# A two-layer encoder trunk on one core: values of the grouped attention one step later, the cast of the last gate in one step with its product, part of a scaling on ScalarE

## The chip, the core and the metric

The kernel runs on one core of a Trainium2 chip. The metric is the device time of one execution in microseconds (us); the time of a kernel is the median of several executions. In the profile PE is TensorE (PEld its weight loads), DVE is VectorE, ACT is ScalarE, POOL is GpSimd and SP is SyncE, which only issues DMAs here.

## What is computed

512 tokens of width 1024 pass through two layers. Both normalize the stream, project it, attend, gate, project back and add the result to the stream:

```
for i in range(2):
    h = rmsnorm(x, norm_g[i]);  proj = h @ w_in
    if i == 0: o_mix = mixer_dilated(q, k, v)      # 3 groups x 8 heads, windows with dilation 1, 4, 16,
                                                   # mixed by a softmax of their log-sum-exps
    else:      o_mix = mixer_axial_gqa(q, k, v)    # 8 query heads, 2 key/value heads, axial rotary
    o_mem = memory_attention(q_mem, rmsnorm(mem))  # 4 heads over 256 memory tokens
    y = concat(o_mix, o_mem) * silu(gate);  x = x + y @ w_out[i]
```

Everything is float32. In layer 1's grouped attention each block of 128 query rows of a head sees all 512 keys.

## The kernel before

**Products.** Float32 accuracy is reached with three matmuls per product: each operand is split into a high part (a cast on ScalarE) and a low part (what is left, a subtraction on VectorE), and `mm3` (L163 to L166) adds high x high (L164), low x high (L165) and high x low (L166) in PSUM. The projections (`s_chunk`, L356) use a scheme in the manner of Strassen with seven instead of eight products of quarters, so that many sums and differences of weights, activations and results are formed on the other engines; L364 copies a product out on ScalarE, L375 and L381 combine products on VectorE.

**Weights.** The class `Weights` (L182) streams the weights in pieces of 128x1024 (512 KB). `dma` (L229) loads them on SP's queue, as many ahead as the table `KEEP` (L39) allows for the kind of the piece: W1b are the seven input projections of layer 1, W2b is the part of its output projection for the memory heads and heads 0 to 3, O1 the part for heads 4 to 7. `sum` (L243) forms sums of pieces by adding DMAs on POOL's queue (L252, L261, L266, L271), `hi` (L278) casts a piece on ScalarE (L287), `lo` (L292) subtracts on VectorE (L297). A cast is taken two slots after its load or sum was issued at the earliest. `advance` (L313) does some of each once per slot.

**The order of the work** is written out by hand. The class `Driver` (L42) counts slots: after every product of a projection TensorE's program calls `tick` (L94), which lets each waiting piece of other work (written as a generator) go one step. `first` work of a slot comes ahead, then generators that finish a product, then at most two steps of attention, and last what was put on the list `late`. `half` (L109) gives the attention a step in the middle of a product. All engines work through their instructions in the order in which they are issued here, and an instruction that waits holds what is behind it on its engine.

**Buffers.** `m4` (L141) hands out tiles of 128x1024 from a pool of 23, for the weights' pieces (wl), keys (kbT), values (vb), queries (qb), transposed probabilities (pbT), gate products (yf, y) and others. `s2` gives tiles of 128x512. Attention uses four PSUM banks (`at`, L150), the projections four (`pj`). A tile or a bank that is handed out again can be written only when its last reader is done.

**Layer 0's attention** (`attn_a`, L1058) works on one head at a time. Two sets of probabilities (o = 0, 1) are formed and multiplied in place by a factor c per row, in which the softmax over the groups lies: c is formed at L1148, `scale(o)` at L1154 to L1157 applies it with four instructions on VectorE, one for each block of 128 rows, and with a second factor of 0.5. Then `turn` (L1159) transposes the set on TensorE, and `pv` multiplies it with the values.

**Layer 1's attention** (`attn_b`, L1356) is a pipeline over 32 blocks of a head's 128 query rows. In a step t, block t has its scores (`score`), block t-1 its exponentials (ScalarE, L1372), t-2 is scaled by its sum (L1379), t-3 is transposed (`turn`, L1388), and the transposed block is cut into a high part (L1392, ScalarE) and a low part (L1397, VectorE). The two blocks of a pair share one pair of pbT tiles, which the first of them takes from the pool. When t-4 is the second block of a pair, `pv` multiplies the pair with the values into a PSUM tile ob, and `out_` copies it (L1413) to o. After two pairs the head is whole and is stored to DRAM (`put_ob`, L1278). The last line of `attn_b` gives the stages with their offsets.

**Gates** (`gates`, L747, for both layers) are three projections: for the memory heads (g = 0), heads 0 to 3 (g = 1) and heads 4 to 7 (g = 2). `ev` finishes a quarter: tanh on ScalarE (L768), the SiLU (L770), the load of the attention's output og (L763) as soon as it is stored, and the multiplication. For g < 2 this is L778 (to yf); `prep_y` (L794) makes the activations of the output projection from them later (casts at L805, subtractions at L806). For g = 2 it is L781, in the next slot the cast to the high part of y (L784), and in the one after it the subtraction for the low part (L786). Then `out_rest` (L728) can multiply these heads with their part of the output weights, the last work of a layer. In layer 1, the last heads' y is what the end of the kernel waits for, behind the attention's last block.

Of the kernel before, what the change touches and what calls it, by code (L numbers as in the profile page):

```python
# [12 lines left out]
AF = mybir.ActivationFunctionType  # L13
ALU = mybir.AluOpType
# [21 lines left out]

SEQ = [1, 2, 0] + list(range(3, len(PLAN)))
T1_DMA = 17
KEEP = {"T2": 8, "T2b": 4, "O1": 4, "W1": 9, "W2": 10, "W2s": 9, "W1b": 7, "W2b": 9}  # L39


class Driver:  # L42
# [83 lines left out]
def trunk_kernel(ctx: ExitStack, tc: tile.TileContext, x, mem, wall, norm_g, mem_norm_g, gcol,  # L126
                 qn_a, kn_a, qn_b, kn_b, ident_d, mask_d, tab_a, tab_b, out):
    nc = tc.nc
    V, A, G, T = nc.vector, nc.scalar, nc.gpsimd, nc.tensor
# [6 lines left out]
    drv = Driver()  # L136
# [610 lines left out]
    def gates(od, o_done):  # L747

        ys, yf, y_done, YW = [None] * 4, [None, None], set(), {}

        def gate(H, first, g, half=False):


            yt = [[m4(F32R, "y").rearrange("p (h t) -> p h t", h=2) for _ in range(2)] for _ in range(2)] if g == 2 else None
            if g < 2:
                yf[g] = [m4(name="yf") for _ in range(2)]

            def ev(q, u, t):
                i, j = int(q[0]) - 1, int(q[1]) - 1
                h0, ts = first + 2 * j, slice(i * 256, (i + 1) * 256)  # L760
                def load():
                    o = s2(name="og")
                    nc.sync.dma_start(o.rearrange("p (h t) -> p h t", h=2), od[h0:h0 + 2, :, ts].rearrange("h p t -> p h t"))  # L763
                    return o

                o = load() if {h0, h0 + 1} <= o_done else None
                th = s2(name="th")
                A.activation(th, t, AF.Tanh, scale=0.5)  # L768
                yield 1
                V.scalar_tensor_tensor(t, th, 1.0, t, ALU.add, ALU.mult)  # L770
                yield 1
                if not o:
                    while not {h0, h0 + 1} <= o_done:
                        yield 1
                    o = load()
                    yield 1
                if g < 2:
                    V.tensor_tensor(yf[g][j][:, i * 512:(i + 1) * 512], t, o, ALU.mult)  # L778
                    y_done.add((g, i, j))
                    return  # L780
                V.tensor_tensor(t, t, o, ALU.mult)  # L781
                yield 1
                tv = t.rearrange("p (h t) -> p h t", h=2)
                A.copy(yt[j][0][:, :, ts], tv)  # L784
                yield 1
                V.tensor_tensor(yt[j][1][:, :, ts], tv, yt[j][0][:, :, ts].bitcast(F32), ALU.subtract)  # L786
                y_done.add((g, i, j))
                if {(2, 0, j), (2, 1, j)} <= y_done:
                    for k in range(2):
                        ys[2 * j + k] = (yt[j][0][:, k], yt[j][1][:, k])  # L790

            s_chunk(256, H, ev, tokens=False, half=half, soon=g == 2)

        def prep_y():  # L794

            def wait(*gi):
                while not {(g, i, j) for g, i in gi for j in range(2)} <= y_done:
                    yield 1

            def put(k, src):  # L800
                t = big(F32R, "y" + k)
                for j in range(2):
                    js = slice(j * 512, (j + 1) * 512)
                    lo = t[:, 1024 + j * 512:1024 + (j + 1) * 512]
                    A.copy(t[:, js], src[j])  # L805
                    V.tensor_tensor(lo, src[j], t[:, js].bitcast(F32), ALU.subtract)  # L806
                YW[k] = t.rearrange("p (a k t) -> p a k t", a=2, k=4)

            while None in yf:
                yield 1  # L810
            a11, a21, a12, a22 = [[yf[g][j][:, i * 512:(i + 1) * 512] for j in range(2)] for g in range(2) for i in range(2)]
            yield from wait((1, 0))
            put("12", a12)
            yield 1
            yield from wait((0, 0))
            put("11", a11)
            yield 1
            yield from wait((0, 1), (1, 1))
            s1 = [s2(name="ys") for _ in range(2)]
            for j in range(2):  # L820
                V.tensor_tensor(s1[j], a21[j], a22[j], ALU.subtract)
            yield 1
            put("S1", s1)
            yield 1
            for j in range(2):
                V.tensor_tensor(s1[j], s1[j], a11[j], ALU.subtract)
            yield 1
            put("S2", s1)
            yield 2
            for j in range(2):  # L830
                V.tensor_tensor(a12[j], a12[j], s1[j], ALU.add)
            yield 1
            put("S4", a12)
            yield 1
            for j in range(2):
                V.tensor_tensor(a21[j], a11[j], a21[j], ALU.subtract)
            yield 1
            put("S3", a21)
            yield 2
            put("22", a22)  # L840

        return gate, prep_y, YW, ys
# [215 lines left out]
    def attn_a(h, qk0, qs, ks, v12, n_done):  # L1058
# [3 lines left out]
        prob = [m4(name="p").rearrange("p (b k) -> p b k", b=4) for _ in range(2)]  # L1062
# [10 lines left out]
        for o in range(2):  # L1073
            new = []
            for b2 in range(2):
                sp = at("sa").rearrange("p (b k) -> p b k", b=2)
                mine = []
                for i in range(2):
                    b = 2 * b2 + i
                    cs = slice(b * 128, (b + 1) * 128)  # L1080
                    if o == 0:
                        lo, hi = max(0, 128 * b - 64), min(S, 128 * b + 192)
                        c0 = lo - (128 * b - 64)
# [61 lines left out]
        rd = sm(8, "rd")  # L1145
        V.reciprocal(rd, dn)
        c = small.tile([128, 2, 4], F32, tag="c", name="c", bufs=2)
        V.tensor_tensor(c.rearrange("p o b -> p (o b)"), e[:, 0], rd, ALU.mult)  # L1148
        yield 1

        pts = {}
# [2 lines left out]
        def scale(o):  # L1154
            for b in range(4):
                c0, c1 = (64 if o == 0 and b == 0 else 0), (192 if o == 0 and b == 3 else 256)
                V.tensor_scalar(prob[o][:, b, c0:c1], prob[o][:, b, c0:c1], c[:, o, b:b + 1], 0.5, ALU.mult, ALU.mult)  # L1157

        def turn(o):  # L1159

# [195 lines left out]
    def attn_b():  # L1356
        sc, pr, pts, tp, rs, oo = {}, {}, {}, {}, {}, {}

        def score(i):
            h, b = divmod(i, 4)  # L1360
            qh, ql = qs_b[h // 4]
            cs = slice(b * 128, (b + 1) * 128)
            sc[i] = at("sb")
            mm3(sc[i], qh[h % 4 // 2][:, h % 2, cs], ql[h % 4 // 2][:, h % 2, cs], kbT[0][:, h // 4], kbT[1][:, h // 4], True, True)

        def top(i):
            pr[i] = sm(1, "nmb"), sm(1, "denb"), sm(1, "rdb"), s2(name="pb")
            V.tensor_reduce(pr[i][0], sc[i], axis=AX.X, op=ALU.max, negate=True)

        def exps(i):  # L1370
            nm, den, rd, pp = pr[i]
            A.activation(pp, sc.pop(i), AF.Exp, bias=nm, accum_out=den)  # L1372

        def recip(i):
            V.reciprocal(pr[i][2], pr[i][1])

        def scale(i):
            _, _, rd, pp = pr[i]
            A.activation(pp, pp, AF.Copy, scale=rd)  # L1379

        def turn(i):
            b2, j = divmod(i, 2)
            pp = pr.pop(i)[3]
            if j == 0:
                pts[b2] = [m4(F32R, "pbT").rearrange("p (k q) -> p k q", k=4) for _ in range(2)]
            tp[i] = at("ptb").rearrange("p (k q) -> p k q", k=4)
            for k in range(4):
                T.transpose(tp[i][:, k, :], pp[:, k * 128:(k + 1) * 128], ident)  # L1388

        def hi(i):  # L1390
            b2, j = divmod(i, 2)
            A.copy(pts[b2][0][:, :, j * 128:(j + 1) * 128], tp[i])  # L1392

        def lo(i):
            b2, j = divmod(i, 2)
            qs = slice(j * 128, (j + 1) * 128)
            V.tensor_tensor(pts[b2][1][:, :, qs], tp.pop(i), pts[b2][0][:, :, qs].bitcast(F32), ALU.subtract)  # L1397

        def pv(i):
            h, b = divmod(i, 4)  # L1400
            if b % 2:
                pT = pts.pop(i // 2)
                o = oo[i] = at("ob")[:, 0:256]
                es = slice(h // 4 * 128, h // 4 * 128 + 128)
                for k in range(4):
                    mm3(o, vb[0][:, k, es], vb[1][:, k, es], pT[0][:, k], pT[1][:, k], k == 0, k == 3)

        def out_(i):
            h, b = divmod(i, 4)
            if b == 1:  # L1410
                rs[h] = put_ob(h)
            if b % 2:
                A.copy(rs[h][:, (b - 1) * 128:(b + 1) * 128], oo.pop(i))  # L1413
            if b == 3:
                put_ob(h, rs[h])

        yield from pipeline(32, (0, score, 0), (4, pv, 0), (3, turn, 0), (2, scale, 0), (1, exps, 0),
                            (0, top, 1), (1, recip, 1), (3, hi, 1), (3, lo, 1), (4, out_, 1),
                            ready=lambda i: n_rot[0] >= 8 + i // 16 * 4)

    for kvh in range(2):
# [134 lines left out]
```

## Time and profile before

| | |
|---|---|
| three executions | 972.17, 972.54, 968.25 us, median 972.17 |
| profiled execution | 966.39 us |
| its span, first to last instruction | 964.6 us |
| granted clock of TensorE, mean | 0.998 |
| groups of weights' splitting on VectorE (L297) | 255 instructions, 314.2 us |
| weights' casts on ScalarE (L287) | 255 instructions, 269.2 us |
| data moved | 209.81 MB, mean 218 GB/s |

The busy time of an engine is the time in which it worked, whatever waited for it. A row of the timeline has the start, the duration, the engine and line, the operation with the tile that it writes and those that it reads, its shape, and in brackets the idle time of the engine ahead of it and what ended that. A row with x2 or x4 stands for so many equal instructions in a row. In the list of waits a row has the waiting engine, tile and line, what it waited for, and then the total, the number and the longest in us. A row of a window has its length and the busy times of PE, PEld, DVE, ACT and POOL with the number of their instructions, the granted clock, the DMA share and the rate. All durations come from the one profiled execution.

### The profile page before, as it was taken

How to read it: one execution, taken by the hardware profiler on the slowest of the kernel's cores; microseconds unless marked ns; L12 is line 12 of the kernel's file. 1: busy time of each engine (PE TensorE's matmuls, PEld its weight loads, DVE VectorE, ACT ScalarE, POOL GpSimd, SP SyncE). 2: the span in 40 equal slices, each digit the busy share in tenths (PEclk: the TensorE clock that was granted, in tenths of full speed). 3: DMA queues.
4: the chain of work that ended last, by engine and by line, in shares of the span. 5: the costliest groups of instructions: out<-in, count | busy, mean ns of one | idle time of the engine just before them, and what ended most of it. 6: DMA issues, size and time to landing. Idle time of an engine off the chain costs nothing.

```text
span 964.6 us, 16613 instructions
## 1 busy us (share of the span) xinstructions
PE 947.5 (98%) x5682; PEld 833.3 (86%) x5682; DVE 790.6 (82%) x1411; ACT 683.0 (71%) x1701; POOL 339.7 (35%) x482
## 2 busy tenths in 40 slices
PE   8999999999999999999999999999899999999998
PEld 5879888888888888888899997888899999998876
DVE  4898676888888888888797999879888997779873
ACT  5874689686868686868675767556778887878760
POOL 1512523556454545464726011323233231011011
PEclk9999999999999999999999999999999999999999
DMA  9799946869686868685858989969976696877744
GB/s 361 234 285 341 288 112 177 288 123 265 147 259 151 258 155 261 154 262 132 269 147 216 276 194 281 310 198 308 284 174 148 175 239 163 222 202 173 191 144 131
DMA packets 89130, 209.81 MB, mean 218 GB/s; under 512 B 25299, under 2 KB 36051, under 8 KB 89045
## 3 DMA queue, kind: packets, MB, share of 16 engines
q1 hardware_dynamic: 69892, 145.76, 43.6%
q0 software_dynamic: 17856, 60.83, 33.7%
q10 hardware_dynamic: 1296, 2.16, 0.6%
q8 instruction: 45, 0.74, 0.3%
q14 instruction: 41, 0.33, 0.1%
HBM read 157.27 MB, written 12.65 MB: 176 GB/s over the span
## 4 chain that ended last, share of the span: by engine, by line
PE 86%; DVE 8%; ACT 3%; DMA 2%; issue 1%; SPq 0%; DVEq 0%; ACTq 0%
PE pj L166 22%; PE pj L164 22%; PE pj L165 22%; DVE wo L297 3%; PE qT L571 2%; PE sa L1089 1%; PE oo L1191 1%; PE pt L1170 1%; PE sa L1085 1%; PE ptb L1388 1%; DMA og<-odb 1%; PE xT L475 1%; PE ob L165 1%; PE row L592 1%; PE ob L166 1%
## 5 line engine op out<-in xcount | busy, mean ns | idle before, releaser
L297 DVE TENSOR_TENSOR wo<-wl,wh 128x1024 fp32r<-128x1024 f32 x255 | 314.2, 1238 | 5.8 <-ACT wh L287 5.7
L287 ACT CAST wh<-wl 128x1024 fp32r<-128x1024 f32 x255 | 269.2, 1059 | 55.9 <-PE pj L166 33.7
L164 PE MATMUL pj<-wh,hS 128*128 128x512 f32 (+1 forms) x448 | 164.3, 367 | 0.0
L165 PE MATMUL pj<-wo,hS 128*128 128x512 f32 (+1 forms) x448 | 158.8, 355 | 4.4 <-DVE wo L297 4.4
L166 PE MATMUL pj<-wh,hS 128*128 128x512 f32 (+1 forms) x448 | 158.7, 354 | 0.0
L164 PE MATMUL pj<-wh,h 128*128 128x512 f32 (+1 forms) x336 | 122.4, 364 | 0.0
L166 PE MATMUL pj<-wh,h 128*128 128x512 f32 (+1 forms) x336 | 118.5, 353 | 0.0
L165 PE MATMUL pj<-wo,h 128*128 128x512 f32 (+1 forms) x336 | 118.4, 352 | 0.1
L424 POOL TENSOR_TENSOR rstd<-mse,half 128x4 f32<-128x4 f32 (+2 forms) x98 | 102.2, 1043 | 8.2
L165 PEld LDWEIGHTS pj<-wo,hS 128*128 128x128 f32 x448 | 85.7, 191 | 15.3 <-DVE wo L297 5.3
L166 PEld LDWEIGHTS pj<-wh,hS 128*128 128x128 f32 x448 | 85.5, 191 | 12.2
L164 PEld LDWEIGHTS pj<-wh,hS 128*128 128x128 f32 x448 | 85.5, 191 | 10.4 <-ACT sn L364 0.4
L364 ACT COPY sn<-pj 128x512 f32<-128x512 f32 x132 | 73.9, 590 | 22.8 <-PE pj L166 19.2
L423 POOL TENSOR_SCALAR mse<-hss 128x4 f32<-128x4 f32 (+1 forms) x86 | 44.1, 513 | 124.0 <-ACT junk L559 120.2
L559 ACT ACTIVATE junk<-sn 128x128 f32<-128x128 f32 x264 | 79.0, 308 | 1.7 <-DVE sn L375 1.7
L1033 POOL TENSOR_TENSOR ta<-sn,tabs 128x128 f32<-128x128 f32 (+1 forms) x64 | 37.0, 579 | 120.0 <-DVE sn L564 91.6
L381 DVE TENSOR_TENSOR sn<-pj,sn 128x512 f32<-128x512 f32 x99 | 67.5, 684 | 5.4 <-PE pj L166 5.0
L166 PEld LDWEIGHTS pj<-wh,h 128*128 128x128 f32 x336 | 63.5, 189 | 8.9
L165 PEld LDWEIGHTS pj<-wo,h 128*128 128x128 f32 x336 | 63.7, 190 | 8.0 <-DVE wo L297 0.8
L164 PEld LDWEIGHTS pj<-wh,h 128*128 128x128 f32 x336 | 63.7, 190 | 7.2
L271 POOL DMA_DIRECT2D wl<-wl x33 | 29.1, 881 | 115.3 <-DVE wo L297 64.4
L164 PE MATMUL pj<-hS,wh 128*128 128x256 f32 x192 | 55.9, 291 | 0.0
(231 smaller groups left out, 2464.3 us busy)
## 6 DMA issues: line engine op xcount, KB each, us to landing
wl<-in_wall_dram SPq DMA_DIRECT2D x222, 512.0 KB, 7.0
wl<-wl POOLq DMA_DIRECT2D x66, 512.0 KB, 6.2
wl<-in_wall_dram POOLq DMA_DIRECT2D x42, 512.0 KB, 8.4
acc<-sn POOLq DMA_DIRECT2D x16, 256.0 KB, 5.2
od<-o SPq DMA_DIRECT2D x12, 256.0 KB, 5.8
og<-od SPq DMA_DIRECT2D x12, 256.0 KB, 6.8
odb<-o SPq DMA_DIRECT2D x12, 256.0 KB, 3.0
og<-odb SPq DMA_DIRECT2D x12, 256.0 KB, 4.5
```

The lines of the kernel that those rows point to most:

```text
L164: T.matmul(o, lh, rh, start=start, stop=False, skip_group_check=True)
L165: T.matmul(o, lh, rl, start=False, stop=False, skip_group_check=True)
L166: T.matmul(o, ll, rh, start=False, stop=stop, skip_group_check=True)
L271: G.dma_start(self.tile[key], self.tile[c, "T2", x], accum_op=ALU.add)
L287: A.copy(wh, self.tile[self.items[i]])
L297: V.tensor_tensor(wo, self.tile[key], wh.bitcast(F32), ALU.subtract)
L364: A.copy(t, b)
L381: V.tensor_tensor(t, b, t, ALU.subtract if q == "12" else ALU.add)
L423: G.tensor_scalar(e, ss, EPS, None, ALU.add)
L424: G.tensor_tensor(r, e, half[:, 0:n], ALU.pow)
L559: A.activation(jk, p[:, j * 128:(j + 1) * 128], AF.Square, scale=QS, accum_out=ss[:, j:j + 1])
L1033: G.tensor_tensor(ta[:, 0:n], xn[:, 0:n, 0:32], ropeA[:, 0, b, s0:s0 + n], ALU.mult)
```

## The change

There are four parts. In `attn_b` the stages `pv` and `out_` come five steps after the scores instead of four. The limit of pieces in flight of the kind W1b falls from 7 to 6. In a gate with g = 2 the cast of the product is put on the list `late` of the slot in which the product is formed, and the `yield` between them goes, so the subtraction comes in the slot after it. In `attn_a` the factor 0.5 goes into c, `scale` has one factor instead of two, and for head 7 ScalarE applies it instead of VectorE.

```diff
-KEEP = {"T2": 8, "T2b": 4, "O1": 4, "W1": 9, "W2": 10, "W2s": 9, "W1b": 7, "W2b": 9}
+KEEP = {"T2": 8, "T2b": 4, "O1": 4, "W1": 9, "W2": 10, "W2s": 9, "W1b": 6, "W2b": 9}
...
                 V.tensor_tensor(t, t, o, ALU.mult)
-                yield 1
                 tv = t.rearrange("p (h t) -> p h t", h=2)
-                A.copy(yt[j][0][:, :, ts], tv)
+                drv.late(lambda: A.copy(yt[j][0][:, :, ts], tv))
                 yield 1
                 V.tensor_tensor(yt[j][1][:, :, ts], tv, yt[j][0][:, :, ts].bitcast(F32), ALU.subtract)
...
-        V.tensor_tensor(c.rearrange("p o b -> p (o b)"), e[:, 0], rd, ALU.mult)
+        V.scalar_tensor_tensor(c.rearrange("p o b -> p (o b)"), e[:, 0], 0.5, rd, ALU.mult, ALU.mult)
...
-                V.tensor_scalar(prob[o][:, b, c0:c1], prob[o][:, b, c0:c1], c[:, o, b:b + 1], 0.5, ALU.mult, ALU.mult)
+                if h == 7:
+                    A.activation(prob[o][:, b, c0:c1], prob[o][:, b, c0:c1], AF.Copy, scale=c[:, o, b:b + 1])
+                else:
+                    V.tensor_scalar(prob[o][:, b, c0:c1], prob[o][:, b, c0:c1], c[:, o, b:b + 1], None, ALU.mult)
...
-        yield from pipeline(32, (0, score, 0), (4, pv, 0), (3, turn, 0), (2, scale, 0), (1, exps, 0),
-                            (0, top, 1), (1, recip, 1), (3, hi, 1), (3, lo, 1), (4, out_, 1),
+        yield from pipeline(32, (0, score, 0), (5, pv, 0), (3, turn, 0), (2, scale, 0), (1, exps, 0),
+                            (0, top, 1), (1, recip, 1), (3, hi, 1), (3, lo, 1), (5, out_, 1),
```

## The prediction, made before the changed kernel had run

> **What bounds the kernel now.** I read the busy times and the chain that ended last on the page, then the waits of TensorE, then the timeline at each of these waits, and last the windows around the three places that the change touches.
>
> ```profile
> span 964.6 us, 16613 instructions
> PE 947.5 (98%) x5682; PEld 833.3 (86%) x5682; DVE 790.6 (82%) x1411; ACT 683.0 (71%) x1701; POOL 339.7 (35%) x482
> PE 86%; DVE 8%; ACT 3%; DMA 2%; issue 1%; SPq 0%; DVEq 0%; ACTq 0%
> ```
>
> TensorE multiplies for 947.5 of 964.6 us. The change takes no matmul away, so all it can win lies in 17.1 us, and much of that is the start and the end. The waits, with the total, the number and the longest:
>
> ```profile
> PE pj L165 <- DVE wo L297: 5.0, 4, 2.9
> PE row L592 <- DMA row<-in_mem_norm_g_dram: 2.4, 1, 2.4
> PE ob L165 <- DVE pbT L1397: 2.2, 2, 1.4
> PE pj L166 <- DVE y L786: 1.0, 1, 1.0
> ```
>
> These name the places: weights that VectorE has not yet split (L297), the low halves of the grouped attention's probabilities (L1397), and the low half of the last gated heads (L786). In order of time:
>
> ```profile
> 592.62 0.50 PE L165 MATMUL pj<-wo,yS 128*128 128x512 f32 x1 [0.57 <-DVE wo L297]
> 594.43 0.50 PE L164 MATMUL pj<-wh,yS 128*128 128x512 f32 x1 [0.39 <-DVE sn L381]
> 678.80 0.39 PE L165 MATMUL pj<-wo,hS 128*128 128x256 f32 x1 [2.85 <-DVE wo L297]
> 873.93 0.39 PE L165 MATMUL ob<-pbT,vb 128*128 128x256 f32 x1 [1.37 <-DVE pbT L1397]
> 912.06 0.38 PE L165 MATMUL ob<-pbT,vb 128*128 128x256 f32 x1 [0.87 <-DVE pbT L1397]
> 940.41 0.50 PE L166 MATMUL pj<-wh,y 128*128 128x512 f32 x1 [1.04 <-DVE y L786]
> ```
>
> The sum is made against the profiled execution, 966.39 us (span 964.6 and 1.79 around it). That is 5.78 under the median of 972.17, so I add the sum's difference to the median. About 0.5%, 4.9 us, is what a measurement here can tell from no change.
>
> **a. The last head's scaling on ScalarE.** In layer 0 the four scalings of each set of head 7 leave VectorE.
>
> ```profile
> 578.80:602.90 24.10, 22.88 (x104) 17.51 (x103) 23.35 (x45) 18.57 (x30) 3.46 (x4) 1.00 0.99 281
> 589.70 1.14 DVE L1157 TENSOR_SCALAR p<-p,c 128x256 f32<-128x256 f32 x4
> 597.23 1.07 DVE L1157 TENSOR_SCALAR p<-p,c 128x192 f32<-128x192 f32 x4
> L691 ACT ACTIVATE pm<-pm,rdm 128x256 f32<-128x256 f32 x32 | 14.6, 509 | 0.0
> 596.15 1.22 ACT L805 CAST yS<-yf 128x512 fp32r<-128x512 f32 x2 [2.29 <-DVE yf L836]
> ```
>
> The window's columns are its length, then PE, PEld, DVE, ACT and POOL busy. VectorE is busy 23.35 of 24.10 us, so it sets the two waits at 592.62 and 594.43 (0.57 + 0.39 = 0.96). Taking 1.14 off just ahead of them removes both: **-0.96** (bounds -0.96 and 0). What hides the other side is ScalarE's idle time, 24.10 - 18.57 = 5.53 us, one piece of it the 2.29 at 596.15. The same operation at the same size, L691, takes 509 ns, and eight make at most 4.07 us. If that cover went, the transposes of head 7 would come late by what does not fit; the values of head 7 are needed only one to three slots on, so I take nothing. The factor 0.5 moves into c, and the other heads' scalings lose their second operation: still one instruction each, in front of which nobody waits, so 0.
>
> [...]
>
> **b. The values one step later.** In the loop over 32 blocks (four of 128 query rows to a head) the values matmuls are issued in the step after the one in which they were. The two waits for L1397 go, because the low half has a step more: **-2.24** (1.37 + 0.87; bounds -2.24 and 0).
>
> **c. What the later values hold.** A pair of blocks has two transposed tiles, a high and a low one. Two pairs are now alive between the turn of the next pair and the values of the last. They come from the pool of 23 tiles that also holds the weights. I count, at step 13: keys 2, values 2, queries 6, weights 9, gate products 2, probabilities 2, which is 23, full; the change makes it 25. The lowered limit of W1b does not help there, since from step 12 on the pieces being loaded are W2b's, with their limit of 9. From step 17 to 23 two query tiles are gone and a gate tile is more: 24. So in the odd steps 13 to 23 a new tile waits until the next step's values have read the old one. One such wait stands in the trace of before, 0.47 us at 840.25. The steps as PE runs them (scores 831.58, values 832.28, transposes 833.71, half a product 834.07, scores 835.58, whole product 836.64 to 839.58):
>
> ```profile
> 831.58 0.40 PE L164 MATMUL sb<-kbT,qb 128*128 128x512 f32 x1
> 832.28 0.28 PE L164 MATMUL ob<-pbT,vb 128*128 128x256 f32 x1
> 833.71 0.60 PE L1388 MATMUL ptb<-ident,pb 128*128 128x128 f32 x4
> 834.07 0.37 PE L164 MATMUL pj<-hS,wh 128*128 128x256 f32 x1
> 835.58 0.40 PE L164 MATMUL sb<-kbT,qb 128*128 128x512 f32 x1
> 836.64 0.36 PE L164 MATMUL pj<-h,wh 128*128 128x256 f32 x1
> 839.58 0.40 PE L164 MATMUL sb<-kbT,qb 128*128 128x512 f32 x1
> 834.35 0.59 ACT L1392 CAST pbT<-ptb 128x512 fp32r<-128x512 f32 x1 [2.11 <-PE ptb L1388]
> 834.97 0.69 DVE L1397 TENSOR_TENSOR pbT<-ptb,pbT 128x512 fp32r<-128x512 f32 x1 [1.73 <-ACT pbT L1392]
> 840.25 0.69 DVE L778 TENSOR_TENSOR yf<-sn,og 128x512 f32<-128x512 f32 x1 [0.47 <-PE sb L165]
> 835.00:868.00 33.00, 33.00 (x257) 31.71 (x256) 23.96 (x40) 26.12 (x52) 4.07 (x5) 1.00 0.71 183
> ```
>
> Scores take 0.70, values 1.43, half a product 1.51, a whole one 2.94. A held L1397 stands for 1.51 + 0.70 + 1.43 = 3.64 us in a half step, 5.07 in a whole one, and behind it on VectorE stand the weights' L297 and the scores' maximum; behind a held L1392 on ScalarE stand the weights' casts L287. TensorE feels it through the four PSUM banks of the attention: two hold scores that ScalarE has not read, one the new values, so the next transposes need the bank of the last ones, and that is free only after L1392 and L1397. At step 13 both are held: 0.59 + 0.69 and a handover of about 0.07, 1.35 us. At 15, 17, 19, 21 and 23 the low half alone is: 0.69 and a handover, 0.75. That is 1.35 + 5 x 0.75 = **+5.10**. The trace of before has no such wait on the probabilities, so the bounds are far apart: 0, if the shortage falls on weight loads, which have time; and 5.10 + 5.07 = 10.2, if on top VectorE ends the stage one hold behind (below). I take the figure worked out from the rows.
>
> **d. The tail.** The last values move one slot back, behind a product, and so do the copy, the store, the load of og and the multiplication. The cast of the last gate (L784) now follows its multiplication in the same slot, and the subtraction comes one slot sooner after it.
>
> ```profile
> 929.21 0.40 PE L164 MATMUL pj<-wh,yS 128*128 128x512 f32 x1
> 931.96 0.39 PE L164 MATMUL pj<-wh,y 128*128 128x512 f32 x1
> 936.05 1.36 DVE L781 TENSOR_TENSOR sn<-sn,og 128x512 f32<-128x512 f32 x2 [4.06 <-DMA og<-odb]
> 936.78 1.29 ACT L784 CAST y<-sn 128x512 fp32r<-128x512 f32 x2 [0.81 <-DVE sn L781]
> 937.33 1.22 DVE L297 TENSOR_TENSOR wo<-wl,wh 128x1024 fp32r<-128x1024 f32 x1
> 938.46 1.28 DVE L375 TENSOR_TENSOR sn<-sn 128x512 f32<-128x512 f32 x2
> 939.67 1.29 DVE L786 TENSOR_TENSOR y<-sn,y 128x512 fp32r<-128x512 f32 x2
> ```
>
> The product behind which they move takes 931.96 - 929.21 = 2.75. The multiplication waits for og (4.06), so it comes 2.75 later. The weights' L297 that stood between it and L786 goes ahead of it, into the wait: 938.46 - 937.33 = 1.13 less. The two L375 stay between, and under them the casts. L786 comes 2.75 - 1.13 = 1.62 later, TensorE needs it when it does now, and its wait grows from 1.04 to 2.66: **+1.62** (bounds -1.04, the whole wait gone, and +2.75). In layer 0 the same cast edit meets no wait of TensorE for L786 (the one in the list is at 940.41): 0.
>
> **e. One W1b piece fewer.**
>
> ```profile
> wl<-in_wall_dram SPq DMA_DIRECT2D x222, 512.0 KB, 7.0
> ```
>
> Each load for layer 1's input projections is issued one slot later on SP's queue, and the sums behind it on POOL's. A load lands in 7.0 us, some 2.4 slots of 2.94, and of the list's four waits for L297 the one at 678.80 is the last, so layer 1's weights come in time. I take **0**; the bound above is one slot at the layer change, +2.94.
>
> **Sum:** -0.96 - 2.24 + 5.10 + 1.62 + 0 = +3.52: 969.9 for the profiled execution, 972.17 + 3.52 = **975.7** on the median.
>
> **The rivals.**
>
> R1, slower: VectorE loses more than the banks show. The holds of 835 to 892 add up to 3 x 3.64 + 3 x 5.07 = 26.1 us, and VectorE has only 33.00 - 23.96 = 9.04 spare in 835 to 868. It can lag TensorE by one step only, since the hold ends with that step. From the point at which this lag eats the lead of the weights' splitting, TensorE waits for L297 too, by one hold: c becomes 10.2, the time 972.17 - 3.20 + 1.62 + 10.2 = 980.8. For it: VectorE's load. Against it: the splitting runs up to two slots ahead.
>
> [...]
>
> R2, the gains are kept: the pool's shortage falls on loads with time to spare, c is 0, and the time 972.17 - 3.20 + 1.62 = 970.6; if the tail's wait also goes, 972.17 - 3.20 - 1.04 = 967.9. For it: one tile is given back by W1b; the pool waits of before cost TensorE nothing. Against it: my count of 25.
>
> R3, the weights come late: one slot at the layer change on top, 975.7 + 2.94 = 978.6. For it: the 2.85 at 678.80 shows no slack in that place.
>
> R4, the later step does not do what it says:
>
> ```profile
> 868.00:892.20 24.20, 22.83 (x144) 20.21 (x144) 23.84 (x39) 21.58 (x41) 3.71 (x5) 1.00 0.71 175
> ```
>
> VectorE is full there (23.84 of 24.20), so the two waits of b come back as waits for something else of VectorE's: 975.7 + 2.24 = 977.9.
>
> **How the numbers follow.** Forecast 0.36, R1 0.20, R2 0.22 (0.06 of it at 967.9), R3 0.10, R4 0.12. Faster means under 967.3, slower over 977.0. Under 967.3 lies the lower edge of R2, with noise of the runs: 0.08. Over it lie R1, most of R3 and R4, and little of the forecast: 0.34. Within: 0.58. The forecast's own range is 973 to 978; from 968 to 981 all cases but the outer halves of R1 and of R2's lower branch are in.
>
> **What would show it.** a: no wait at 592 and 594, L1157 on ScalarE. b: no wait of ob for L1397. c: L1392 and L1397 waiting for ob's matmuls, and ptb for L1397, every second step from about 835; without such rows c is wrong and R2 holds. Waits for L297 between 835 and 892 speak for R1, one that is longer near 679 for R3. d: L786's wait about 2.7. It would be wrong altogether if the time fell under 968, which needs c at nothing and the tail's wait gone.

## The result and the profile after

The changed kernel takes 979.59 us (median of 6 executions, 977.57 to 980.30), the kernel before 970.23 us beside it (6 executions, 968.09 to 974.64). The ratio is 1.0095, with a 95% interval of 1.0068 to 1.0122: slower, by about 9.2 us. The prediction's number was 975.7. The time lies in its wide range of 968 to 981, but outside the forecast's own 973 to 978, and above 977.0, the side to which the prediction gave 0.34. The profiled execution of the changed kernel took 979.55 us. Line numbers of the changed kernel differ by one or two from those before: L1399 is the low half of the probabilities (before L1397), L1394 the high half (L1392), L1390 the transposes (L1388), L785 the low half of y (L786).

From the page of the changed kernel, the span and the busy times:

```profile
span 977.8 us, 16614 instructions
PE 952.3 (97%) x5682; PEld 836.6 (86%) x5682; DVE 788.9 (81%) x1403; ACT 685.3 (70%) x1709; POOL 341.3 (35%) x482
```

TensorE has the same 5682 matmuls and is busy 4.8 us longer (952.3 against 947.5); a part of them, behind the layer change, ran at a lower clock (0.50 from 688.5 to 694.5, below). The rest of the 13.2 us between the two spans is idle time of TensorE. Its waits (total, number, longest):

```profile
PE pj L165 <- DVE wo L297: 6.2, 4, 2.9
PE pj L164 <- ACT hS L539: 3.6, 1, 3.6
PE ptb L1390 <- DVE pbT L1399: 3.6, 5, 1.3
...
PE pj L164 <- DVE sn L381: 1.4, 2, 1.1
PE pj L166 <- DVE y L785: 1.1, 1, 1.1
```

Two large groups are new: the wait for hS, which is ScalarE's cast of layer 1's first activations, and the five waits of the transposes for L1399. The waits for L381 have grown from 0.4 to 1.4 us, and three single waits of 0.4 to 0.8 us are new too. The two waits of the values (ob) for the low half are gone, the wait for L785 at the end is there still. The timeline puts them in place:

```profile
581.21 0.50 PE L165 MATMUL pj<-wo,y 128*128 128x512 f32 x1 [1.80 <-DVE wo L297]
...
597.14 0.50 PE L164 MATMUL pj<-wh,yS 128*128 128x512 f32 x1 [1.08 <-DVE sn L381]
...
680.53 0.39 PE L165 MATMUL pj<-wo,hS 128*128 128x256 f32 x1 [2.87 <-DVE wo L297]
688.63 0.55 PE L164 MATMUL pj<-wh,hS 128*128 128x256 f32 x1 [3.59 <-ACT hS L539]
...
848.55 0.65 PE L1390 MATMUL ptb<-ident,pb 128*128 128x128 f32 x4 [1.29 <-DVE pbT L1399]
865.80 0.66 PE L1390 MATMUL ptb<-ident,pb 128*128 128x128 f32 x4 [0.72 <-DVE pbT L1399]
882.73 0.66 PE L1390 MATMUL ptb<-ident,pb 128*128 128x128 f32 x4 [0.72 <-DVE pbT L1399]
...
953.59 0.50 PE L166 MATMUL pj<-wh,y 128*128 128x512 f32 x1 [1.06 <-DVE y L785]
```

Where the 13.2 us arise can be read by setting equal instructions of the two timelines side by side: the first scores of the grouped attention and its last transposes, before

```profile
778.06 0.48 PE L164 MATMUL sb<-kbT,qb 128*128 128x512 f32 x1
...
924.57 0.60 PE L1388 MATMUL ptb<-ident,pb 128*128 128x128 f32 x4
```

and after:

```profile
786.29 0.48 PE L164 MATMUL sb<-kbT,qb 128*128 128x512 f32 x1
...
937.70 0.60 PE L1390 MATMUL ptb<-ident,pb 128*128 128x128 f32 x4
```

The first waiting matmul of layer 1's projections stands at 678.80 before and at 680.53 after: 1.7 us were lost in layer 0. The first scores come 8.23 us later, so 6.5 of these arose at the layer change. The last transposes come 13.13 later, 4.9 more, in the attention: between these two rows TensorE waits 2.95 us longer, and the same 1015 matmuls keep it busy 1.95 us longer, at a granted clock of 1.00 in both kernels. What follows them takes the same in both. The largest part is thus where the prediction had 0.

The layer change, on the queue that issues the summing DMAs, before:

```profile
654.02 0.94 POOL L252 DMA_DIRECT2D wl<-in_wall_dram  x1
662.96 0.93 POOL L261 DMA_DIRECT2D wl<-wl  x1
...
671.78 0.87 POOL L271 DMA_DIRECT2D wl<-wl  x1 [6.97 <-DVE fS L531]
```

and after:

```profile
664.56 0.94 POOL L252 DMA_DIRECT2D wl<-in_wall_dram  x1
675.53 0.87 POOL L261 DMA_DIRECT2D wl<-wl  x1 [10.03 <-DVE hS L540]
...
684.30 0.87 POOL L271 DMA_DIRECT2D wl<-wl  x1 [6.97 <-DMA wl<-wl]
```

The first sum goes out 10.5 us later (664.56 - 654.02). Of these, 1.7 were lost in layer 0 already, so one slot later means 8.8 us at this place, not 2.94. The second sum, which needs the first, goes from 662.96 to 675.53. On ScalarE of the changed kernel the cast of that piece then waits, and the cast of hS stands behind it:

```profile
683.65 1.04 ACT L287 CAST wh<-wl 128x1024 fp32r<-128x1024 f32 x1 [5.03 <-DMA wl<-wl]
684.60 0.61 ACT L539 CAST hS<-f 128x512 fp32r<-128x512 f32 x1
```

TensorE waits 3.59 us for it and then runs slowly for six more. Two windows of the changed kernel show it; the granted clock is the third number from the end, ahead of the DMA share and the rate, 0.50 and then 0.97:

```profile
688.50:694.50 6.00, 5.87 (x27) 5.90 (x28) 4.35 (x6) 3.70 (x13) 0.00 (x0) 0.50 0.93 214
694.50:700.00 5.50, 5.50 (x47) 5.50 (x46) 4.27 (x6) 3.16 (x6) 3.59 (x4) 0.97 0.85 258
```

In the attention, the rows that wait for the values' matmuls are the holds that the prediction spoke of; after the values of the next step ScalarE or VectorE goes on:

```profile
847.19 0.59 ACT L1394 CAST pbT<-ptb 128x512 fp32r<-128x512 f32 x1 [3.85 <-PE ob L165]
858.20 0.69 DVE L1399 TENSOR_TENSOR pbT<-ptb,pbT 128x512 fp32r<-128x512 f32 x1 [4.00 <-PE ob L165]
865.05 0.69 DVE L1399 TENSOR_TENSOR pbT<-ptb,pbT 128x512 fp32r<-128x512 f32 x1 [1.53 <-PE ob L165]
875.44 0.69 DVE L1399 TENSOR_TENSOR pbT<-ptb,pbT 128x512 fp32r<-128x512 f32 x1 [3.70 <-PE ob L165]
881.99 0.69 DVE L1399 TENSOR_TENSOR pbT<-ptb,pbT 128x512 fp32r<-128x512 f32 x1 [1.83 <-PE ob L165]
```

### The profile page after: what moved, and what is told of

Same layout as the page of the kernel before. It is cut to its first block, busy times and chain, and to the rows that moved or that the text cites. A ratio compares the mean times of both kernels' runs of the same rounds, so it can differ in the third digit from the quotient of the medians.

```text
span 977.8 us, 16614 instructions
## 1 busy us (share of the span) xinstructions
PE 952.3 (97%) x5682; PEld 836.6 (86%) x5682; DVE 788.9 (81%) x1403; ACT 685.3 (70%) x1709; POOL 341.3 (35%) x482
## 5 line engine op out<-in xcount | busy, mean ns | idle before, releaser
L297 DVE TENSOR_TENSOR wo<-wl,wh 128x1024 fp32r<-128x1024 f32 x255 | 314.4, 1239 | 7.9 <-ACT wh L287 7.7
L287 ACT CAST wh<-wl 128x1024 fp32r<-128x1024 f32 x255 | 269.3, 1059 | 69.0 <-PE pj L166 34.3
L164 PEld LDWEIGHTS pj<-wh,hS 128*128 128x128 f32 x448 | 87.0, 194 | 14.2 <-issue 3.8
L166 PEld LDWEIGHTS pj<-wh,hS 128*128 128x128 f32 x448 | 86.7, 194 | 12.2
L381 DVE TENSOR_TENSOR sn<-pj,sn 128x512 f32<-128x512 f32 x99 | 67.6, 685 | 5.4 <-PE pj L166 5.0
L271 POOL DMA_DIRECT2D wl<-wl x33 | 29.3, 889 | 102.8 <-DVE wo L297 53.3
L261 POOL DMA_DIRECT2D wl<-wl x33 | 31.2, 980 | 81.2 <-DMA wl<-in_wall_dram 21.3
```

Source lines behind the costliest of these rows:

```text
L164: T.matmul(o, lh, rh, start=start, stop=False, skip_group_check=True)
L166: T.matmul(o, ll, rh, start=False, stop=stop, skip_group_check=True)
L261: G.dma_start(self.tile[key], self.tile[c, "T1", x], accum_op=ALU.add)
L287: A.copy(wh, self.tile[self.items[i]])
L297: V.tensor_tensor(wo, self.tile[key], wh.bitcast(F32), ALU.subtract)
L381: V.tensor_tensor(t, b, t, ALU.subtract if q == "12" else ALU.add)
```

## The experiments

The theory after the result: the limit of W1b costs its whole loss at the layer change (about 6 us), the later values cost about 5 us because the pool of 23 tiles is too small for them, the scaling gains about 1 us, and the cast loses a little in layer 0. The rival: the limit is harmless, what is late at 688 was late already, and the later values cost little by themselves. Ratios are to the kernel before, which ran beside each; 0.1% is about 1 us. The diffs are shortened to what they do.

**The limit alone.**

```diff
-"W1b": 7
+"W1b": 6
```

> The kernel before with one part of the change, the limit of W1b pieces at 6 instead of 7. Theory: the limit alone makes the loss at the layer change. After it the first sums of layer 1's weights go out one slot later, ScalarE's cast L287 waits some 5 us for a summing DMA, the cast of hS (L539) stands behind it, TensorE waits about 3.6 us for it near 688, and its next matmuls come slower, some 2.6 us more: +5 to +6.5 us. Rival (the prediction's step e): the loads have time to spare, 0 within 1 us, and the wait near 688 of the changed kernel comes from what was late before it in layer 0.

Measured: 977.28 us, ratio 1.0082 (1.0062 to 1.0103), about 7.9 us. The second sum is issued at 674.96 as in the changed kernel, and on this kernel's ScalarE the cast waits for it:

```profile
682.32 1.05 ACT L287 CAST wh<-wl 128x1024 fp32r<-128x1024 f32 x1 [4.13 <-DMA wl<-wl]
```

TensorE's timeline of the same kernel has two waits that the kernel before has not:

```profile
687.31 0.55 PE L164 MATMUL pj<-wh,hS 128*128 128x256 f32 x1 [4.19 <-DVE sn L381]
794.28 0.41 PE L164 MATMUL pj<-hS,wh 128*128 128x256 f32 x1 [1.86 <-ACT wh L287]
```

The rival falls: the limit by itself delays the sums, the cast and TensorE (at 687 the profile names L381, a combination of products that comes behind that cast on VectorE, as the last to come). The loss is above the expected 5 to 6.5; the wait at 794 is a second one that the limit makes, and the whole change has only 0.34 us there.

**The cast alone.**

```diff
                 V.tensor_tensor(t, t, o, ALU.mult)
-                yield 1
...
-                A.copy(yt[j][0][:, :, ts], tv)
+                drv.late(lambda: A.copy(yt[j][0][:, :, ts], tv))
```

> The kernel before with the cast of the last gate in its product's slot, nothing else. Theory: in layer 0 the cast stands on ScalarE behind a VectorE that is full, holds the weights' casts and L805 up for 2 to 3 us, and TensorE waits near 581 for L297 (about 1.8 us in place of none) and runs slower for some us after it: +2 to +3.5 us there; in layer 1 the wait for L786 at the end shrinks by up to 1.0 us; together +1 to +2.5 us. Rival (the prediction's step d): nothing in layer 0, so 0 to -1.0 us, and the wait near 581 comes from the scaling on ScalarE.

Measured: 971.57 us, ratio 1.0017 (1.0000 to 1.0033), 1.6 us, at the edge of its uncertainty and in the expected 1 to 2.5. Its profile has two waits where the kernel before has none, of 0.68 and 0.29 us:

```profile
579.69 0.50 PE L165 MATMUL pj<-wo,y 128*128 128x512 f32 x1 [0.68 <-DVE wo L297]
582.99 0.50 PE L165 MATMUL pj<-wo,y 128*128 128x512 f32 x1 [0.29 <-DVE wo L297]
```

On ScalarE of this kernel the cast holds all that is behind it until VectorE has formed the product:

```profile
572.63 0.62 ACT L783 CAST y<-sn 128x512 fp32r<-128x512 f32 x1 [4.06 <-DVE sn L781]
```

This hold, 4.06 to 5.17 us long, stands in all four profiles with the cast edit in layer 0 and in none of the ten without it. In the same four a wait for L381 near 596 is 0.98 to 1.38 us, and in the other ten at most 0.39. In this one it is

```profile
596.16 0.50 PE L164 MATMUL pj<-wh,yS 128*128 128x512 f32 x1 [0.98 <-DVE sn L381]
```

So the cast has a price in layer 0, which the prediction had at nothing. How much of the 1.80 us at 581 in the changed kernel is the cast's is open: waits of 0.8 to 1.3 us at this place also stand in profiles of kernels without the cast (below: the values alone). In layer 1 the cast alone does gain: the wait of 1.04 us for the low half of y at the end is gone from this profile, so the price in layer 0 is nearer 2.6 than 1.6 us (an estimate, 1.6 + 1.04).

**The scaling alone.**

```diff
-c = e * rd;  V.tensor_scalar(prob, prob, c, 0.5, ALU.mult, ALU.mult)
+c = e * 0.5 * rd;  h == 7: A.activation(prob, prob, AF.Copy, scale=c), else V.tensor_scalar(prob, prob, c, None, ALU.mult)
```

> The kernel before with head 7's scaling on ScalarE and the factor 0.5 in c, nothing else. Theory (the prediction's step a): the two waits near 592 and 594 go, about -1.0 us, and no wait near 581. Rival: ScalarE's eight scalings (4 us) hold its copies of the products and casts, so that the waits stay or grow by about a microsecond: 0 to +1 us; or they make the wait near 581 of the changed kernel: +2 to +3 us.

Measured: 968.01 us, ratio 0.9984 (0.9968 to 1.0000), -1.5 us, at the edge of its uncertainty. Of the two waits near 592 and 594 one is left, shorter:

```profile
592.27 0.50 PE L164 MATMUL pj<-wh,yS 128*128 128x512 f32 x1 [0.31 <-DVE sn L381]
```

**The values alone**, with a limit that the layer change does not feel (7 for the first of the seven input projections, 6 for the others).

```diff
-... + ["W1b"] * 7 + ...
+... + ["W1c"] + ["W1b"] * 6 + ...        # KEEP: "W1c": 7, "W1b": 6
-(4, pv, 0) ... (4, out_, 1)
+(5, pv, 0) ... (5, out_, 1)
```

> The kernel before with the values one step later, and a limit of 7 pieces for the first of layer 1's seven input projections and 6 for the others, so that the layer change loads as before and the rest as after. Theory: the two waits of the values for L1397 go (-2.2 us), the transposes wait for L1397 about five times (3.6 us) and TensorE runs slower after each wait; the changed kernel lost 4.9 us between its first scores and its last transposes: +4 to +5 us, no wait of 3.6 us near 688. Rival: most of these 4.9 us are a consequence of the late weights, and the values alone cost less than 2 us or win.

Measured: 976.33 us, ratio 1.0073 (1.0049 to 1.0098), 7.1 us; the waits of the transposes are those of the whole change, to 0.01 us:

```profile
848.90 0.66 PE L1388 MATMUL ptb<-ident,pb 128*128 128x128 f32 x4 [1.29 <-DVE pbT L1397]
866.13 0.66 PE L1388 MATMUL ptb<-ident,pb 128*128 128x128 f32 x4 [0.72 <-DVE pbT L1397]
883.08 0.66 PE L1388 MATMUL ptb<-ident,pb 128*128 128x128 f32 x4 [0.72 <-DVE pbT L1397]
```

More than the 4 to 5 expected. The profiled execution was its slowest (981.08) and lost some 7 us before layer 1, where its program does what the kernel before does; and the limit of 6 for the last six projections is in it (next).

**The limit of 6 for the last six projections only.** W1c is a kind like W1b with a limit of its own.

```diff
-["W1b"] * 7                      # "W1b": 7
+["W1c"] + ["W1b"] * 6            # "W1c": 7, "W1b": 6
```

> The kernel before with the limit of 6 for the last six of the seven input projections only, the first keeps 7. Theory: almost all of the limit's 7.9 us lies at the layer change: 0 to +2 us here (the run with the limit alone had one more new wait, 1.9 us for L287 near 794, with slow matmuls after it). Rival: the loss is spread over the seven projections: +4 us or more.

Measured: 972.81 us, ratio 1.0032 (1.0008 to 1.0056), about 3 us, more than the 0 to 2 expected. Its profile has the wait for L287 again (1.72 us at 793). The limit costs most at the first projection, and something at the others.

**The whole change with 7 for the first projection.** To the changed kernel:

```diff
-["W1b"] * 7                      # "W1b": 6
+["W1c"] + ["W1b"] * 6            # "W1c": 7, "W1b": 6
```

> The whole change, but with a limit of 7 pieces for the first of layer 1's seven input projections (6 for the other six). Theory: the loss at the layer change is made by the limit at that place alone, so the first sum (L252) goes out a slot earlier again, the waits of ScalarE for the summing DMA and of TensorE for hS near 688 go, and the whole change costs about 9.3 - 6 = 3 us more than the kernel before (2 to 5). Rival: the values' shift pays about 7 us by itself, as its own run had it, and the sum of the parts holds: +6 us or more.

Measured: 974.07 us, ratio 1.0039 (1.0023 to 1.0055), 3.8 us, in the expected 2 to 5. One piece more at one place takes 5.5 us off the 979.59 of the change. The wait for hS is gone, and on the queue of the summing DMAs the first two sums are back in their places:

```profile
654.96 0.94 POOL L252 DMA_DIRECT2D wl<-in_wall_dram  x1
664.30 0.93 POOL L261 DMA_DIRECT2D wl<-wl  x1 [0.47 <-issue]
```

**Room for the later values**: as the values alone, and W2b limited to 7 pieces, so that two tiles come free at step 13.

```diff
-"W2b": 9
+"W2b": 7
```

> The values one step later with the limits 7 and 6 as in the run of the values alone, and W2b limited to 7 pieces instead of 9, which makes room for the second pair of probabilities (25 - 2 = 23 tiles at step 13). Theory: the transposes' waits for L1397 from step 13 on go (1.29, 0.72 and 0.72 us near 849, 866 and 883), the two waits of the values stay away, and it is 2 to 5 us faster than the run of the values alone, if loading two pieces fewer costs nothing (the control shows that). Rival: the waits are not the pool's, and stay.

**Its control**, the kernel before with only W2b at 7.

> The kernel before with W2b limited to 7 pieces instead of 9, nothing else: the control for the run with room. Theory: no difference beyond 1 us, since two pieces are two slots of lead out of about four. Rival: the loads of the output projection's pieces come late, TensorE waits for L297 or L287 between 840 and 920: +2 us or more.

Measured: with room 969.32 us, ratio 0.9988 (0.9971 to 1.0005); without it 1.0073. The control takes 972.35 us, 1.0030 (1.0014 to 1.0046): fewer pieces in flight alone cost 2 to 3 us, more than expected. So the room is worth about 8 us to the later values, more than the expected 2 to 5, although it costs something by itself. The profiles show 4.4 us of this between the first scores and the last transposes (152.63 us without room, 148.20 with it); where the rest lies is not shown. Of the waits in the attention none is left after step 12 in the kernel with room; what remains there are these three:

```profile
786.12 0.36 PE L164 MATMUL pj<-hS,wh 128*128 128x256 f32 x1 [2.18 <-ACT wh L287]
794.76 0.65 PE L1388 MATMUL ptb<-ident,pb 128*128 128x128 f32 x4 [0.39 <-DVE pbT L1397]
805.02 0.39 PE L164 MATMUL ob<-pbT,vb 128*128 128x256 f32 x1 [0.77 <-DVE qb L1334]
```

That the shortage in the pool makes the three waits at 849, 866 and 883 is shown: same order of work, two tiles freed, and the waits and the holds behind them are gone, while the control shows no gain from fewer weights in flight. The two waits of the values for the low half stay away as well, so the step that the prediction had as gain is a gain.

**The whole change with both repairs.** To the whole change with 7 for the first projection:

```diff
-"W2b": 9
+"W2b": 7
```

> The whole change with both repairs: 7 pieces for the first input projection, 7 instead of 9 for W2b. Theory: what the change lost are the layer change (gone with the first repair) and the pool (gone with the second), so it is at the kernel before within 2 us, at best 2 us faster, and some 4 to 5 us faster than the change with the first repair alone. Rival: the cast in layer 0 or the tail keeps a loss, +2 us or more.

Measured: 967.67 us, ratio 0.9982 (0.9963 to 1.0001): with both causes removed the change is no loss, and some 5.5 us better than with the first repair alone (0.9982 against 1.0039). The limit and the pool are enough to explain the 9.2 us.

**A better version.** Values later, the scaling on ScalarE, no cast edit, and to these

```diff
-["W1b"] * 7                      # "W1b": 7, "W2b": 9
+["W1c"] * 4 + ["W1b"] * 3        # "W1c": 7, "W1b": 6, "W2b": 7; in the second run * 6 and * 1
```

> The values one step later with W2b limited to 7 and head 7's scaling on ScalarE; W1b's limit is 7 for the first four input projections of layer 1 and 6 for the last three. Theory: the wait for L287 near 786 (2.2 us with 6 for the last six) goes, the transposes do not wait for L1397 after step 12, the two waits of the values are gone and so are those near 592: 2 to 5 us faster than the kernel before. Rival: the seventh piece brings the pool's shortage back into steps 3 to 12, and it is no faster than the run with room.

> As the run before it in this call, but with 7 for the first six input projections and 6 for the last one only. Theory of the pool: at steps 5 to 11 the count is 2 + 2 + 8 + 7 + 1 or 2 + 4 = 24 or 25 tiles, so that waits of the transposes or values for the pool appear between 795 and 835: 1 to 3 us slower than the run before it. Rival: the count is not what decides, and both are the same within 0.5 us.

Measured: 968.05 us, ratio 0.9982 (0.9962 to 1.0003), and 964.26 us, ratio 0.9948 (0.9928 to 0.9968). The first gains less than the expected 2 to 5 us. The second was expected to be slower and is the fastest kernel of the study, about 5 us under the kernel before. TensorE's timeline of it has one wait in the attention:

```profile
802.37 0.38 PE L164 MATMUL ob<-pbT,vb 128*128 128x256 f32 x1 [0.69 <-DVE qb L1337]
```

So my count of tiles does not foretell the steps before 12: with more pieces allowed there, a wait of the transposes at step 4 (0.40 us at 793.52 with four projections at 7) is gone with six. Why is not settled.

**The cast in layer 1 alone**, on the version with four projections at 7.

```diff
                 V.tensor_tensor(t, t, o, ALU.mult)
-                yield 1
-                A.copy(yt[j][0][:, :, ts], tv)
+                layer 0: yield 1; A.copy(yt[j][0][:, :, ts], tv)
+                layer 1: drv.late(lambda: A.copy(yt[j][0][:, :, ts], tv))
```

> The run with room and scaling (four projections with 7), and also the cast in its product's slot in layer 1 alone. Theory (the prediction's step d): the wait for L786 at the end, about 1.06 us with the later values, shrinks or stays, 0 to -1 us. Rival: 0, since what ends last there is the load of og, and the cast follows the product anyway.

Measured: 967.55 us, ratio 0.9986 (0.9970 to 1.0001) against 0.9982 without: no difference. The wait at the end is 1.09 us, and 1.05 without. With the values where they were the same edit took this wait away (the cast alone): there the low half of y follows its product and one L297 on VectorE, with the later values the two L375 go ahead of it.

## Why the prediction was right or wrong

**What bounds the kernel**: right. TensorE's matmuls stayed, and every loss that was placed is a wait of TensorE or matmuls that take longer around one.

**a, the scaling**, -0.96: right for the scaling alone, -1.5 with an interval that reaches 0 and a wait of 0.31 left. In the whole change this gain does not show: the wait for L297 is gone, but the one for L381 is 1.08 us at 597.14 where it was 0.39, together as long as the 0.96 of before. By the count of profiles above, that is the cast edit's doing, which the prediction had at 0 in layer 0.

**b, the values' own waits**, -2.24: right. Both waits are gone in every kernel with the later values.

**c, the pool**, +5.10: the mechanism was right and is shown; the size was not worked out rightly. Five of six holds came (847 to 882), the first with both halves, and the first wait of the transposes was 1.29 where 1.35 was worked out, the others 0.72 for 0.75. But only three of six came (849, 866, 883): at 858 and 875 the low half was held 4.00 and 3.70 us across a whole product, and the transposes did not wait, so they did not need its bank, as I had taken for every step. On the other side stand waits that I did not have: of the transposes at 803 and 903 (0.39 and 0.45), of the values at 814 and 891 (0.77 and 0.39). The attention as a whole lost 4.9 us in the profiles, against 5.10 - 2.24 = 2.9 forecast. Its waits alone grew by 2.95 us, so that their sum came out is luck, missing ones against others; the 1.95 us by which the matmuls took longer stood in no term. R1, with VectorE a whole hold behind and waits for L297, did not come: no such wait stands between 835 and 892, and VectorE stood still for 11.1 us in four holds, where R1 counted 26.1. The holds of every second step reached TensorE only at every fourth (849, 866, 883).

**d, the tail**, +1.62: wrong, 0.0 (1.04 before, 1.06 after). The term that failed is the time of og's load. SP's queue at the end, before:

```profile
930.23 0.38 SPq L238 DMA_DIRECT2D wl<-in_wall_dram  x1
931.90 0.99 SPq L763 DMA_DIRECT2D og<-odb  x2
```

and after; then, from VectorE's timeline after, the product that waits for the load:

```profile
947.73 0.89 SPq L763 DMA_DIRECT2D og<-odb  x2
```

```profile
950.36 1.36 DVE L781 TENSOR_TENSOR sn<-sn,og 128x512 f32<-128x512 f32 x2 [1.53 <-DMA og<-odb]
```

From the load's issue to the product it was 936.05 - 931.90 = 4.15 us before and is 950.36 - 947.73 = 2.63: 1.5 of the 2.75 us come back. Before, a weight of 512 KB had gone out just ahead; one slot later none is left to load. That this is the reason is read from the rows and was not tried. The cast edit, taken as 0 in layer 0, cost 1.6 us alone, with the 1.04 us that it gained at the end already in that figure.

**e, the limit**, 0 with +2.94 as bound: this step failed, and it is the largest. The prediction took a slot at 2.94 us, the length of a product in the attention's stage, and no slack as the exception (R3). At the layer change a slot was 8.8 us long, and the late sums made TensorE wait 3.59 us and then run for 6 us at a granted clock of 0.50; the whole term is 5.5 us by the repair (979.59 to 974.07), 7.9 alone. I had its row at hand in the 2.85 us at 678.80, which showed that this place had no slack, and gave it a chance of 0.10.

**The sum**: 3.5 us forecast, 9.2 measured. That the time still lies in the range of 968 to 981 is partly luck: the range stands on 972.17, and the kernel before took 970.23 beside the change; 9.2 us on top of 972.17 would be 981.4. In the profiles the places add up, 1.7 in layer 0, 6.5 at the layer change, 4.9 in the attention and 0 behind it, to 13.1 of the 13.2 us between the spans. That is more than the 9.2 between the medians, because the profiled execution of before, 966.39 us, was faster than any of the six of the comparison (968.09 at least), and because layer 0's 1.7 us are within what single executions differ by there: up to 684 and 686 us, where the kernel before is at 678.80, in runs that change nothing in layer 0. That the parts alone add up to more than the whole (0.82, 0.73 and 0.17% less 0.16%) has one cause that the runs show: the values alone already hold the limit of 6 for six projections (0.32%). The rest is not resolved.

## What to carry to other kernels

Here one piece in flight fewer was not paid in pieces but in slots of the place where it binds (8.8 us at the layer change, where 2.94 was taken): look for the longest slot, and for the place that already waits (2.85 us at 678.80). Before a stage is moved later, count what its tiles keep alive in the pools it draws from (the shortage made waits of 1.29, 0.72 and 0.72 us here), and in what order the instructions behind a held one are needed on its engine (on ScalarE the cast of hS came right behind one that had waited 5.03 us); then give the room at the same time. A change with four parts can hide two gains under two losses: here the later values and the scaling gain 5 us once the limit is mostly put back and the room is made.

## What the runs showed of the hardware

After some waits TensorE's matmuls ran slower for a while, so that these waits cost more than their length, and after others they did not. After 3.59 us of waiting at 688.63 the next six microseconds ran at a granted clock of 0.50: 27 matmuls in 6.0 us, where 47 took 5.5 us right after them, some 2.7 us lost on top. The wait of 2.83 to 2.87 us at the layer change stands in all profiles but one (4.22 with the values alone); by the distances between equal matmuls (0.21 us, and 0.12 further on) it was followed by a slow stretch worth 1.5 us in the kernel before (granted clock 0.66 from 679 to 684) and by none in the profiles of the cast alone and of W2b alone (1.00). The shortest wait with a slow stretch after it was one of 1.08 us in the run of the values alone (with 0.61 shortly before it), while waits of 2.18 and 2.76 us in the runs with room and with W2b alone had none. After waits of 1.08 to 1.86 us the granted clock was in some places 0.57 to 0.62 over the next 4 us, as in the changed kernel after the 1.80 us at 581.21 (0.62), and in others 1.00, as there after the 1.08 us at 597.14 and the 1.29 us at 848.55. So the length of a wait alone did not decide here whether the matmuls after it ran slower; what did was not shown. In the attention of the changed kernel the clock stayed at 1.00 and the same matmuls still took 1.95 us longer; why is open.
